# Layer 0 without a norm in front: transposed input times the gain goes into the projections, the root of the mean square is applied where they leave PSUM

## The chip, the core and the metric

The kernel runs on one core of one Trainium2 chip. The metric is the device time of one execution in microseconds (us); the times given are medians of several executions. The engines are TensorE (PE, matmuls, with its weight loads PEld), VectorE (DVE), ScalarE (ACT), GpSimd (POOL) and SyncE (SP), which here issues nearly all transfers. Each runs its own instructions in the order in which they were written, and waits for others by semaphores.

## What is computed

Two layers over 1024 tokens of width 1024, all in float32. The part that the change touches is the front of layer 0:

```python
def rms_norm(x, g):
    xf = x.astype(jnp.float32)
    y = xf * lax.rsqrt(jnp.mean(xf * xf, axis=-1, keepdims=True) + NORM_EPS)
    return (y * g.astype(jnp.float32)).astype(x.dtype)

h = rms_norm(x, norm_g[0])                       # layer 0
q, k, v, gate = jnp.split(h @ w_in, 4, axis=-1)  # mixer A: 16 heads of 64, each 1024 wide
# neighbourhood attention over a 16 x 64 grid: each query sees 8 x 16 keys, plus a bias per head
y = (o * silu(gate)) @ w_out
x = x + y
g = sigmoid(rms_norm(x, ple_norm_g[0]) @ ple_w_gate[0])
x = x + g * (p[0] @ ple_w_proj[0])
```

Layer 1 has the same frame with grouped-query attention, and one more norm ends the program. With r(t) = 1/sqrt(mean(x(t)^2) + eps) for token t, h(t) = r(t) * (x(t) * g), so that h @ w = r(t) * ((x * g) @ w): the factor r may be applied before the projection or behind it.

## The kernel before, in words

Every float32 product is made of three passes over operands split in a high and a low part: `HTh`, `HTl` hold the (normed) input transposed, [channel, token tile, channel block, token], and each weight unit of 128 x 1024 (512 KB) is split into `wh`, `wl`. The high part is made by ScalarE (a rounding copy), the low part by VectorE (the difference). `mm` (L303) issues all matmuls; `split3` is the three passes.

Weight units come through a queue, `Weights`: SP loads a unit into one of two staging buffers (`wstage`, L203), `pump` splits it (L218, L219). `pump` is called after each item of work, so transfers and splits are woven into the order in which the code is written; nothing else schedules.

`mixer_a` (layer 0) begins with the norm, by token tile t = 0..7 of 128 tokens: load `X[t]` [token, channel] (`load`, L694), ScalarE squares it with a running sum (`square`, L697), a mean on VectorE (L701), a power -1/2 on POOL (`rsqrt_ops`, L311), the scaling by r and gain (`scale`, L713 on VectorE or L715 and L716 on ScalarE and POOL), and eight PE transposes into PSUM, from where ScalarE and VectorE write `HTh` and `HTl` (`to_ht`, L413 to L415). Between these steps stand the projections of the first four heads' V, tile by tile (`v_items`, evictions L567 and L568). Then come q and k of head 0, transposed, in two halves of 512 tokens (`qk_items`, `qk_evac`: L581 copies PSUM to `th`, then `QS`, `KA`, `KB` are made; L590 and L593 copy halves of `KA` and `KB` across partitions).

Then the attention: for each head 8 steps of scores (`f_S`), exponent (`f_E`), transposes (`f_T`) and the product with V (`f_AV`). `mix` weaves the next head's q and k projections and the gate's (`gate_items`, L508) into them by cost. `table(h+1)` builds the next head's bias table on POOL (L612) from rows `u` that SP loads (L609) in step 1 of each head. These rows come from a table in DRAM that is built at the start by 8 and 16 small transfers (L748, L766). At the end of a head pair POOL multiplies the output with the gate and with the inverse row sums (`fin`, L499, L500), the latter spread by a trip through DRAM (L436, L438). Some steps are put off by a number of items with `post.add`; the q/k evictions' three steps by `QD = (2, 5, 8)`.

The first score matmul of head 0 is the first PE instruction behind the q and k of head 0.

## Time and profile before

| | |
|---|---|
| median of 3 runs | 1562.63 us (1560.91 to 1562.86) |
| the profiled execution, its own time | 1564.6 us |
| its span, from the first to the last instruction | 1562.8 us |
| mean granted TensorE clock | 0.997 |
| instructions | 23940 |

The page of a profile gives busy time by engine, then the span in 40 equal slices (a digit is the busy share in tenths). A timeline's row reads: start, duration, engine, line of the kernel, operation, output<-inputs, partitions x elements, how often, and in brackets how long the engine sat idle before it and what ended that. A row of a line's view gives the duration in ns as least/median/greatest, and the first and last start. A group's row (x31 | 18.4, 595 | 18.8 ...) gives the count, busy us, mean ns, and idle us before it with what ended it. A row of stretches gives start:end, length, then busy us (and instructions) of PE, PEld, DVE, ACT, POOL, the granted clock, the busy share of the DMA engines and GB/s.

### The profile page before, as it was taken

The numbers are of one execution on the slowest core, as the hardware profiler recorded it, in microseconds if no ns is written. First come the engines' busy times: TensorE is split into PE (matmuls) and PEld (weight loads), VectorE is DVE, ScalarE is ACT, GpSimd is POOL, SyncE is SP. The second block draws the span as 40 slices with busy tenths as digits, with TensorE's granted clock in tenths as the row PEclk, the third lists the DMA queues.
The fourth block names the chain that finished last, engine by engine and source line by source line (L and its number), as shares of the span: only waits on it lengthen the run. The fifth ranks groups of instructions, "written<-read, shape, count | busy, mean of one in ns | idle before, by whom it ended". The sixth has DMA issues, their size and how long they took to land.

```text
span 1562.8 us, 23940 instructions
## 1 busy us (share of the span) xinstructions
PE 1520.8 (97%) x9048; PEld 1328.0 (85%) x9048; DVE 965.3 (62%) x1660; ACT 871.6 (56%) x1744; POOL 320.3 (20%) x409
## 2 busy tenths in 40 slices
PE   6999999999999999999999999999999999999998
PEld 6888988988988788888988889989899888778886
DVE  5566576476467434536767776677777777624533
ACT  6565465466366523433566776776767777622422
POOL 3102102112012010000433142553141400000124
PEclk9999999999999999999999999999999999999999
DMA  8211222132122962132210111101101213651113
GB/s 288 83 40 53 66 67 78 40 93 79 40 80 83 340 237 90 53 130 104 77 49 22 38 51 42 59 24 55 50 27 46 77 39 107 233 202 54 68 59 130
DMA packets 89859, 138.82 MB, mean 89 GB/s; under 512 B 16913, under 2 KB 55953, under 8 KB 89745
## 3 DMA queue, kind: packets, MB, share of 16 engines
q1 hardware_dynamic: 85136, 122.62, 23.9%
q10 hardware_dynamic: 4608, 14.68, 2.6%
q8 instruction: 71, 1.16, 0.3%
q14 instruction: 44, 0.35, 0.1%
HBM read 104.65 MB, written 36.15 MB: 90 GB/s over the span
## 4 chain that ended last, share of the span: by engine, by line
PE 81%; ACT 6%; DVE 6%; issue 3%; POOL 2%; DMA 2%; SPq 0%; ACTq 0%; POOLq 0%; DVEq 0%
PE d L303 54%; PE o L303 10%; PE s L303 8%; PE t L1057 6%; PE t L654 2%; DVE PTl L1060 2%; PE t L413 2%; DVE mn L1041 1%; DMA wstage<-in_wts 1%; ACT PTh L1059 1%; ACT wh L218 1%; ACT P L1047 1%; POOL xn L402 1%; DVE wl L219 1%; POOL tb L612 1%
## 5 line engine op out<-in xcount | busy, mean ns | idle before, releaser
L303 PE MATMUL d<-wh,HTh 128*128 128x256 f32 (+1 forms) x1096 | 372.3, 340 | 4.9 <-ACT HTh L414 2.6
L303 PE MATMUL d<-wh,HTl 128*128 128x256 f32 (+1 forms) x1096 | 365.7, 334 | 1.5 <-DVE HTl L415 1.5
L303 PE MATMUL d<-wl,HTh 128*128 128x256 f32 (+1 forms) x1096 | 365.2, 333 | 0.0
L1060 DVE TENSOR_TENSOR PTl<-t,PTh 128x512 fp32r<-128x512 f32 x256 | 164.4, 684 | 123.4 <-ACT PTh L1059 122.8
L303 PEld LDWEIGHTS d<-wh,HTh 128*128 128x128 f32 x1096 | 207.7, 189 | 28.4 <-ACT HTh L414 3.2
L303 PEld LDWEIGHTS d<-wh,HTl 128*128 128x128 f32 x1096 | 207.7, 189 | 23.8 <-DVE HTl L415 2.1
L303 PEld LDWEIGHTS d<-wl,HTh 128*128 128x128 f32 x1096 | 208.0, 190 | 21.4
L303 PE MATMUL d<-HTh,wh 128*128 128x512 f32 x504 | 206.1, 409 | 0.0
L303 PE MATMUL d<-HTl,wh 128*128 128x512 f32 x504 | 197.7, 392 | 0.0
L303 PE MATMUL d<-HTh,wl 128*128 128x512 f32 x504 | 197.7, 392 | 0.0
L1047 ACT ACTIVATE P<-s,mn 128x1024 f32<-128x1024 f32 x128 | 142.8, 1115 | 58.3 <-DVE mn L1041 57.7
L1059 ACT ACTIVATE PTh<-t 128x512 fp32r<-128x512 f32 x256 | 139.9, 594 | 43.2 <-PE t L1057 42.3
L1041 DVE TENSOR_REDUCE mn<-s 128x1 f32<-128x1024 f32 x128 | 154.7, 1209 | 11.7 <-PE s L303 11.5
L1057 PE MATMUL t<-ident,P 128*128 128x128 f32 x1024 | 137.4, 275 | 6.7 <-DVE PTl L1060 4.8
L219 DVE TENSOR_TENSOR wl<-wstage,wh 128x1024 fp32r<-128x1024 f32 x89 | 113.8, 1284 | 39.9 <-ACT wh L218 39.4
L1057 PEld LDWEIGHTS t<-ident,P 128*128 128x128 f32 x1024 | 114.7, 141 | 22.5 <-DVE PTl L1060 16.5
L303 PE MATMUL s<-KA,QS 128*128 128x512 f32 (+2 forms) x384 | 133.7, 402 | 0.0
L303 PE MATMUL o<-PTh,V 128*128 128x256 f32 (+2 forms) x672 | 119.0, 288 | 3.3 <-ACT PTh L657 1.7
L303 PE MATMUL s<-KB,QS 128*128 128x512 f32 (+2 forms) x384 | 121.8, 371 | 0.0
L303 PE MATMUL o<-PTl,V 128*128 128x256 f32 (+2 forms) x672 | 119.5, 289 | 0.4 <-DVE PTl L658 0.3
L658 DVE TENSOR_TENSOR PTl<-t,PTh 128x384 fp32r<-128x384 f32 (+1 forms) x128 | 66.6, 520 | 79.3 <-ACT PTh L657 78.3
L303 PEld LDWEIGHTS d<-HTh,wl 128*128 128x128 f32 x504 | 94.6, 188 | 22.0
(159 smaller groups left out, 2456.7 us busy)
## 6 DMA issues: line engine op xcount, KB each, us to landing
wstage<-in_wts SPq DMA_DIRECT2D x92, 512.0 KB
X<-in_x SPq DMA_DIRECT2D x16, 512.0 KB
pp<-ppD SPq DMA_DIRECT2D x32, 256.0 KB
rb<-rD SPq DMA_DIRECT2D x56, 128.0 KB
ppD<-th SPq DMA_DIRECT2D x24, 256.0 KB
xD<-X SPq DMA_DIRECT2D x8, 512.0 KB
X<-xD SPq DMA_DIRECT2D x8, 512.0 KB
yD0h<-rb SPq DMA_DIRECT2D x14, 256.0 KB
```

Source lines behind the costliest of these rows:

```text
L218: act.activation(hi, s, AF.Copy)
L219: self.rest = lambda: dve.tensor_tensor(lo, s, hi, ALU.subtract)
L303: pe.matmul(ps, a, b, start=first, stop=last, skip_group_check=True)
L402: pool.tensor_scalar(xns[i][:, :512], xts[i][:, :512], r[:, i:i + 1], None, op0=ALU.mult)
L413: pe.transpose(ps[:, k], xn[:, (4 * c + k) * 128:(4 * c + k + 1) * 128], ident)
L654: pe.transpose(ps[:, i], sp[:, i * 128:(i + 1) * 128], ident)
L658: dve.tensor_tensor(PTl[:, sl], ps[:, :m], PTh[:, sl], ALU.subtract)
L1041: dve.tensor_reduce(mn, ps, axis=AX.X, op=ALU.min)
L1047: act.activation(p, ps, AF.Exp, bias=mn, scale=-1.0, accum_out=RS[h, hf][:, t:t + 1])
L1057: pe.transpose(ps[:, i], p[:, k * 128:(k + 1) * 128], ident)
L1059: act.activation(PTh[:, ks, c], ps, AF.Copy)
L1060: dve.tensor_tensor(PTl[:, ks, c], ps, PTh[:, ks, c], ALU.subtract)
```

## The change

The host now also gives x transposed (`xT`, channel by token), the gain of layer 0 as a column per channel block (`gain0`), and the bias rows per head ready made (`bias`) in place of the bias table.

The start of `mixer_a` is written anew. `put` multiplies a block of x^T by the gain per channel and writes the high part (ScalarE) and the low part (VectorE) of `HTh`, `HTl`, with neither norm nor transpose. The x tiles [token, channel] are still loaded, into four buffers, for the squares; `roots` makes r of four tiles at once (`rt`, a column per token tile), and `spread` transposes r on PE and copies it into `R` [any partition, token]. V of the first four heads is projected by halves of 512 tokens, channel block by channel block into two banks (`v_first`), and r comes in at the eviction (`v_evac`). Six times four transposes of the identity stand at PE's start. q, k and gates take R at their eviction, which moves from ScalarE to VectorE; the two copies across partitions move from VectorE to POOL. Each head's bias rows are loaded in step 0 and turned into the table in step 3.

```diff
-        "x": tokens(g["x"][0]), "wts": W, "rpb": rpb, "gains": gains, "hgains": hg,
+        "x": tokens(g["x"][0]), "xT": tokens(g["x"][0]).reshape(1024, 1024).T.reshape(8, 128, 1024), "wts": W, "bias": bias, "gains": gains, "gain0": g["norm_g"][0].reshape(8, 128).T, "hgains": hg,
...
+        def split_now(self, pieces):
+            key, pid = self.q[self.split]
+            s, _ = self.st.pop(key)
+            hi, lo = self.alloc[pid]()
+            for a, b in chunks(1024, 1024 // pieces):
+                act.activation(hi[:, a:b], s[:, a:b], AF.Copy)
+                dve.tensor_tensor(lo[:, a:b], s[:, a:b], hi[:, a:b], ALU.subtract)
...
     def gate_items(key, pair, hf, alloc, sb, gg, R=None):
...
-            act.activation(G, ps, AF.Copy)
+            if R is None:
+                act.activation(G, ps, AF.Copy)
+            else:
+                dve.tensor_tensor(G, ps, R[:, hf * 512:(hf + 1) * 512], ALU.mult)
...
+            def v_evac(t):
+                def evac(ps):
+                    v = ps.rearrange("p (h d) -> p h d", h=4)
+                    act.activation(V[:, t, :, 0:64], v, AF.Copy, scale=rt[:, t:t + 1])
+                    dve.scalar_tensor_tensor(V[:, t, :, 64:128], v, rt[:, t:t + 1], V[:, t, :, 0:64], op0=ALU.mult, op1=ALU.subtract)
+                return evac
...
+            def v_first(hf, banks, k):
+                wh, wl = WQ.get(("av", 0, k // 4))
+                c = slice((k % 4) * 256, (k % 4 + 1) * 256)
+                for i in range(3):
+                    for t in range(4):
+                        a = (HTh, HTh, HTl)[i][:, 4 * hf + t, k, :]
+                        mm(banks[t // 2][:, (t % 2) * 256:(t % 2 + 1) * 256], a, (wh, wl, wh)[i][:, c],
+                           k == 0 and i == 0 and t % 2 == 0, k == KC - 1 and i == 2)
...
-                    act.activation(raw, ps, AF.Copy)
+                    dve.tensor_tensor(raw, ps, R[:, s], ALU.mult)
...
-                        dve.tensor_copy(ka[lo, s], ka[hi, s])
+                        pool.tensor_copy(ka[lo, s], ka[hi, s])
...
-                        dve.tensor_copy(kb[lo, s], kb[hi, s])
+                        pool.tensor_copy(kb[lo, s], kb[hi, s])
...
+            def put(hf, k):
+                src = XT[hf][k // 2][:, k % 2].rearrange("p (t c) -> p t c", t=4)
+                ts = slice(4 * hf, 4 * hf + 4)
+                act.activation(HTh[:, ts, k, :], src, AF.Copy, scale=g0[:, k:k + 1])
+                dve.scalar_tensor_tensor(HTl[:, ts, k, :], src, g0[:, k:k + 1], HTh[:, ts, k, :], op0=ALU.mult, op1=ALU.subtract)
+
             def square(t):
-                act.activation(junk, X[t], AF.Square, accum_out=stat[:, 0, t:t + 1])
+                junk = ini.tile([128, D], BF16, name="junk")
+                act.activation(junk, X[t], AF.Square, accum_out=stat[:, t:t + 1])
...
+            def roots(hf):
+                c = slice(4 * hf, 4 * hf + 4)
+                dve.tensor_scalar(stat[:, c], stat[:, c], 1.0 / D, EPS, op0=ALU.mult, op1=ALU.add)
+                pool.tensor_tensor(rt[:, c], stat[:, c], neghalf[:, 0:4], ALU.pow)
+
+            def spread(hf):
+                ps = talloc()
+                for i in range(4):
+                    pe.transpose(ps[:, i], rt[:, 4 * hf + i:4 * hf + i + 1].to_broadcast([128, 128]), ident)
+                act.activation(R[:, hf * 512:(hf + 1) * 512], ps.rearrange("p t c -> p (t c)"), AF.Copy)
...
+            for i in range(6):
+                ps = talloc()
+                for j in range(4):
+                    pe.transpose(ps[:, j], ident, ident)
+            put(0, 0)
+            put(0, 1)
+            WQ.split_now(2)
+            put(0, 2)
+            put(0, 3)
+            WQ.split_now(1)
+            for k in range(4, KC):
+                put(0, k)
+            banks = [dalloc(), dalloc()]
+            for k in range(KC):
+                v_first(0, banks, k)
...
+            for t in range(4):
+                square(t)
+            roots(0)
+            for k in range(4):
+                put(1, k)
+            for t in range(4):
+                v_evac(t)(banks[t // 2][:, (t % 2) * 256:(t % 2 + 1) * 256])
+            for k in range(4, KC):
+                put(1, k)
+            WQ.split_now(1)
+            for t in range(4, NT):
+                square(t)
+            roots(1)
...
-            for d in qk_items(0):
+            for i, d in enumerate(qk_items(0)):
                 d[0]()
+                if i == 1:
+                    spread(1)
                 WQ.pump()
...
-                        if j == 1 and h + 1 < NH:
-                            table(h + 1)
+                        if h + 1 < NH:
+                            if j == 0:
+                                US[0] = bias_in(h + 1)
+                            if j == 3:
+                                table(h + 1, US[0])
```

From the last head pair's end on, the instructions of every engine stand in the same order as before. Where the order changes, three places are shown. SP, the start of the program, before (`X` is x by token tile, `gain` the broadcast gain, `wstage` a weight unit):

```order
L694 DMA X_109<-in_x 128x1024
L722 DMA gain<-in_gains 128x1024
L694 DMA X_110<-in_x 128x1024
L203 DMA wstage<-in_wts 128x1024 x2
L694 DMA X_111<-in_x 128x1024
L694 DMA X_112<-in_x 128x1024
```

SP, the same place, now (`g` is the gain by channel, `XT` two channel blocks of x^T for 512 tokens):

```order
L755 DMA g_110<-in_gain 128x8
L728 DMA XT_112<-in_xT 128x2x512
L205 DMA wstage<-in_wts 128x1024
L728 DMA XT_113<-in_xT 128x2x512
L205 DMA wstage<-in_wts 128x1024
L728 DMA XT_114<-in_xT 128x2x512
L728 DMA XT_115<-in_xT 128x2x512
L732 DMA X<-in_x 128x1024 x4
L728 DMA XT_116<-in_xT 128x2x512
```

The x tiles moved behind the first half of x^T and the two weight units of V. ScalarE, the start, before (`junk` is the square's output that nobody reads, `HTh` an eviction of transposes):

```order
L697 ACTIVATE junk,stat<-X_110 128x1024
L218 ACTIVATE wh_140<-wstage 128x1024
L218 ACTIVATE wh_146<-wstage 128x1024
L414 ACTIVATE HTh<-t 128x512 x2
L697 ACTIVATE junk,stat<-X_111 128x1024
L697 ACTIVATE junk,stat<-X_112 128x1024
```

ScalarE, the same place, now (`HTh<-XT,g` is `put`):

```order
L737 ACTIVATE HTh<-XT_112,g_110 128x4x128 x2
L232 ACTIVATE wh_178<-wstage 128x512 x2
L737 ACTIVATE HTh<-XT_113,g_110 128x4x128 x2
L232 ACTIVATE wh_188<-wstage 128x1024
L737 ACTIVATE HTh<-XT_114,g_110 128x4x128 x2
L737 ACTIVATE HTh<-XT_115,g_110 128x4x128 x2
L742 ACTIVATE junk,stat<-X 128x1024 x4
L737 ACTIVATE HTh<-XT_116,g_110 128x4x128 x2
L737 ACTIVATE HTh<-XT_117,g_110 128x4x128 x2
L583 ACTIVATE V<-d,rt 128x4x64 x4
```

The squares moved from in front of the first operands to between the two halves of them. POOL in the attention, before: the tables of heads 4 and 5 (`tb`) and the products at the end of the head pair before them (`Y`, one pair of rows for each half of the tokens); the like returns with the later heads:

```order
L612 TENSOR_TENSOR tb<-MK,u 128x128 x10
L499 TENSOR_TENSOR Y<-Y,G 128x512
L500 TENSOR_TENSOR Y<-Y,rb 128x512
L499 TENSOR_TENSOR Y<-Y,G 128x512
L500 TENSOR_TENSOR Y<-Y,rb 128x512
```

POOL, the same products and head 5's table, now (`KA`, `KB` are the copies across partitions for head 5, a pair for each half of its tokens):

```order
L513 TENSOR_TENSOR Y<-Y,G 128x512
L514 TENSOR_TENSOR Y<-Y,rb 128x512
L644 TENSOR_TENSOR tb<-MK,u 128x128 x5
L619 COPY KA<-KA 64x512
L622 COPY KB<-KB 64x512
L513 TENSOR_TENSOR Y<-Y,G 128x512
L514 TENSOR_TENSOR Y<-Y,rb 128x512
L619 COPY KA<-KA 64x512
L622 COPY KB<-KB 64x512
```

The copies moved into this queue, the first half's pair in front of the second pair of `Y` rows, the second half's behind it; and the table of head 5 stands behind the first pair.

136 lines of the change are left out of this document (54 added, 82 removed).

## The prediction

> **What bounds the kernel now.** I read the page first, for which engine fills the span.
>
> ```profile
> PE 1520.8 (97%) x9048; PEld 1328.0 (85%) x9048; DVE 965.3 (62%) x1660; ACT 871.6 (56%) x1744; POOL 320.3 (20%) x409
> ...
> PE   6999999999999999999999999999999999999998
> ...
> PEclk9999999999999999999999999999999999999999
> ```
>
> TensorE (PE) is busy 97% of the span, and in the row of forty slices of 39 us each only the first falls to 6. So two places can give time: the start, and the few microseconds of idle PE in the layer-0 attention behind it, the only other stage that the change edits. Next the start by stretches of 5 us (busy time of each engine, then clock, DMA share and GB/s):
>
> ```profile
> 0.00:5.00 5.00, 0.00 (x0) 0.00 (x0) 0.00 (x0) 2.15 (x2) 0.77 (x7) 1.00 0.66 185
> 5.00:10.00 5.00, 1.97 (x8) 1.57 (x8) 1.50 (x3) 2.49 (x5) 0.55 (x1) 1.00 1.01 400
> 10.00:15.00 5.00, 3.32 (x14) 3.09 (x15) 4.56 (x6) 4.22 (x7) 0.56 (x1) 1.00 1.02 419
> 15.00:20.00 5.00, 5.00 (x43) 4.84 (x42) 2.84 (x5) 4.38 (x8) 2.95 (x2) 1.00 1.08 356
> ...
> 30.00:40.00 10.00, 8.70 (x74) 8.50 (x73) 9.08 (x11) 5.69 (x10) 3.16 (x1) 1.00 0.91 278
> ```
>
> PE does 0, 2.0, 3.3 and 5.0 us of work in the four stretches, while from 5 us on the DMA share is full at 400 to 419 GB/s. (The last row is wanted further down.) Then the timeline of the start (start, duration, engine, line; in brackets the idle time before and what ended it):
>
> ```profile
> 4.13 1.06 ACT L697 ACTIVATE junk<-X 128x1024 bf16<-128x1024 f32 x1 [2.13 <-DMA X<-in_x]
> ...
> 7.61 1.06 ACT L697 ACTIVATE junk<-X 128x1024 bf16<-128x1024 f32 x1 [2.33 <-DMA X<-in_x]
> ...
> 7.75 1.97 PE L413 MATMUL t<-ident,X 128*128 128x128 f32 x8 [7.75 <-DVE X L713]
> ...
> 10.09 1.06 ACT L218 ACTIVATE wh<-wstage 128x1024 fp32r<-128x1024 f32 x1 [0.18 <-DMA wstage<-in_wts]
> ...
> 11.68 0.58 PE L303 MATMUL d<-wh,HTh 128*128 128x256 f32 x1 [1.96 <-ACT HTh L414]
> ...
> 13.22 0.41 PE L303 MATMUL d<-wh,HTl 128*128 128x256 f32 x1
> ...
> 13.43 0.41 PE L303 MATMUL d<-wh,HTh 128*128 128x256 f32 x1
> ```
>
> The first x tile is there by 4.13, the second (third in the queue) by 7.61, the second weight unit (fifth) by 10.06. PE gets its first transposes at 7.75, after square, root and scaling of tile 0, and its first projection matmul at 11.68. These first matmuls start 0.21 us apart (13.22, 13.43); later ones do better:
>
> ```profile
> 16.03 0.28 PE L303 MATMUL d<-wh,HTl 128*128 128x256 f32 x1
> ...
> 16.15 0.28 PE L303 MATMUL d<-wh,HTh 128*128 128x256 f32 x1
> ...
> 35.57 0.38 PE L303 MATMUL d<-wh,HTl 128*128 128x256 f32 x1 [1.30 <-DVE HTl L415]
> ...
> 45.78 0.40 PE L303 MATMUL d<-HTh,wh 128*128 128x512 f32 x1
> ...
> 56.69 0.28 PE L303 MATMUL s<-KA,QS 128*128 128x256 f32 x1
> ```
>
> From 16.0 us on V matmuls start 0.12 us apart. There is a stall of 1.30 us at 35.57, and 8 transposes stand in front of every token tile. V ends at 45.78, the 48 matmuls of head 0's q and k take 45.78 to 56.69 (0.227 each), and the first score matmul starts at 56.69. That is the mark I carry through: everything in front of it is rewritten, and what PE does behind it is the same list of matmuls.
>
> **The change, part by part.** All durations are of the one profiled execution (span 1562.8, its own time 1564.6, so 1.8 us lie around the span). The rows for the new steps are these:
>
> ```profile
> L697 ACT ACTIVATE junk<-X x8: 1054/1057/1066, 4.1 to 22.2; 128x1024 bf16<-128x1024 f32 x8
> L697 ACT ACTIVATION_READ_ACCUMULATOR junk<-X x8: 186/187/208, 5.1 to 23.2; 128x1 f32 x8
> L715 ACT ACTIVATE X<-X,stat x3: 1152/1152/1156, 16.5 to 29.4; 128x1024 f32<-128x1024 f32 x3
> L218 ACT ACTIVATE wh<-wstage x7: 1048/1057/1068, 8.8 to 58.8; 128x1024 fp32r<-128x1024 f32 x7
> L219 DVE TENSOR_TENSOR wl<-wstage,wh x6: 1209/1222/3077, 9.9 to 48.5; 128x1024 fp32r<-128x1024 f32 x6
> L415 DVE TENSOR_TENSOR HTl<-t,HTh x64: 675/691/694, 11.7 to 1484.6; 128x512 fp32r<-128x512 f32 x64
> L567 ACT ACTIVATE V<-d x32: 364/384/392, 21.0 to 432.3; 128x256 fp32r<-128x256 f32 x32
> 24.25 1.01 POOL L311 TENSOR_TENSOR stat<-stat,neghalf 128x4 f32<-128x4 f32 x1 [3.32 <-DVE stat L701]
> ```
>
> *Arrivals.* The queue now holds the small gain, x^T piece 0, V weights 0, x^T 1, V weights 1, x^T 2 and 3, four x tiles, four x^T pieces, head 0's weights, four x tiles: 19 pieces of 512 KB. The 4 KB in front costs one issue, some 0.45 us, so the first piece lands at 4.6; as before, the third comes 3.5 later and the rest every 1.23 ((10.06 - 7.61)/2, near 524 KB at 419 GB/s, 1.25). That gives weights 0 at 6.3, x^T 1 at 8.1, weights 1 at 9.3, the last x^T of the first half at 11.8, the fourth x tile at 16.7, x^T of the second half from 17.9 to 21.6, head 0's weights at 22.9, the last x tile at 27.8. Unknown is whether x^T, read in 2 KB pieces out of 4 KB rows, keeps that pace. Best: 1.23. Worst by a near row: 278 GB/s at share 0.91 in the stretch 30 to 40 us, where the bias tables move in pieces of 1.5 KB and less, so 305 GB/s and 1.72 us per x^T piece. I take 1.23: the fast stretches carry x, gain and weight tiles of 512 KB each, and an x^T piece is one transfer of that size.
>
> *First half of V.* x^T times gain and the split cost 0.6 to 0.7 us on ScalarE (half of L715's 1.15 is 0.58, plus fixed cost) and 0.69 on VectorE (L415). They don't wait for a root. The weights are split in two halves, 0.6 each, so PE starts at 6.3 + 0.6 = 6.9 in place of 11.68. It then needs 96 matmuls x 0.12 = 11.5 us, to 18.4. Nothing stops it on the way: the last put ends at about 11.8 + 3 x 0.7 = 13.9 and is needed at 17.0; the second weight unit's low half ends at 9.3 + 1.06 + 1.23 = 11.6, needed at 12.7.
>
> *Second half of V.* ScalarE takes the four squares ahead of it: 16.7 + 1.06 + 0.19 = 17.95, then the first put, 18.65. PE starts there, 0.25 us late, and runs 11.5 us, plus four transposes that spread r (0.5): 30.65. ScalarE meanwhile does 8 puts (5.6), 4 V evictions (L567, 1.5), a weight unit (1.06) and 4 squares (5.0): 31.1. VectorE's 0.16 and POOL's root of four columns (L311, 1.01) bring the second half's r at 32.4; PE asks for it after the first 12 q/k matmuls, at 33.4. One microsecond of slack, no cost.
>
> *Head 0.* 10.9 us of q and k matmuls and 0.5 for the second spread: first score at 42.05. The new reader of PSUM there, VectorE times R, is 0.69 where ScalarE took 0.60, and the copies end about 3.5 us after the first half's last matmul; 5.4 us of the second half cover that. Against 56.69 the start gives **14.6 us**: 4.8 by starting earlier, the other 9.8 from 64 transposes taken out (8 put in), stalls and half-speed matmuls. The 24 transposes of the identity cost nothing: at the slow 0.21 they take 5.0 us, and PE has nothing else before 6.9.
>
> *Steady state.* From the first score to 505 us:
>
> ```profile
> 56.69:505.00 448.31, 442.23 (x2542) 386.24 (x2540) 283.18 (x635) 260.64 (x579) 77.67 (x103) 1.00 0.21 64
> ```
>
> 448.31 less 442.23 leaves 6.1 us of idle PE. That bounds the gain there. Per head the change moves work between engines:
>
> ```profile
> L581 ACT ACTIVATE th<-d 128x512 f32<-128x512 f32 x31 | 18.4, 595 | 18.8 <-PE d L303 18.6
> L590 DVE CAST KA<-KA 64x512 fp32r<-64x512 f32 x31 | 15.5, 501 | 1.0
> L957 POOL CAST KA<-KA x8: 607/610/967, 769.8 to 1045.4; 64x512 fp32r<-64x512 f32 x8
> L612 POOL TENSOR_TENSOR tb<-MK,u 128x128 f32<-128x128 f32 x75 | 35.7, 511 | 333.5 <-DMA u<-U 255.5 <-DVE PTl L658 39.0 <-DVE Y L429 28.9
> ```
>
> ScalarE loses three evictions of 0.60 per head (-1.8), VectorE gains three of about 0.69 and loses four copies of up to 0.50 (-2.0): nothing, nearly. POOL gains four copies of 0.61: +2.4 of about 28 us. On VectorE the evictions queue behind other work, but ScalarE's rows show 18.6 us of waiting for PE, so the two buffers have room: one is wanted again only 24 matmuls (5.4 us) later. The bias rows are asked for at step 0 and used at step 3, where before POOL slept on them:
>
> ```profile
> 117.14 3.06 POOL L612 TENSOR_TENSOR tb<-MK,u 128x128 f32<-128x128 f32 x5 [35.14 <-DMA u<-U]
> 120.16 1.48 POOL L499 TENSOR_TENSOR Y<-Y,G 128x512 f32<-128x512 f32 x1
> 121.71 1.43 POOL L500 TENSOR_TENSOR Y<-Y,rb 128x512 f32<-128x512 f32 x1
> ...
> 124.83 0.55 PE L654 MATMUL t<-ident,sp 128*128 128x128 f32 x3 [1.29 <-ACT sp L646]
> ```
>
> Here the table was held by its transfer, the two Y products came behind it, ScalarE behind those, and PE lost 1.29 us. That knot alone is a fifth of the 6.1. With the rows early, the Y products are next to be late only when their own row sums come late. POOL's queue is what I checked for a new wait:
>
> ```profile
> 318.37 0.42 DVE L593 CAST KB<-KB 64x512 fp32r<-64x512 f32 x1
> ...
> 322.16 1.30 POOL L500 TENSOR_TENSOR Y<-Y,rb 128x512 f32<-128x512 f32 x1 [8.89 <-DMA rb<-rD]
> ...
> 323.55 0.36 PE L303 MATMUL s<-KA,QS 128*128 128x256 f32 x1
> ```
>
> Head 9's K copy ends at 318.79 and is wanted at 323.55: 4.8 us of slack. The POOL copies add 2 x 0.19, and a table in front of them 5 x 0.51 = 2.6: still in time. The Y product that waits until 322.16 for its transfer stands behind this copy in the new order. So the gain lies between -3.4 (copies behind that wait: 323.46 + 1.22 = 324.68, 1.1 late, at heads 5, 9 and 13) and 6.1; I take **1.0**, somewhat less than the knot shown: the order excludes the low end, and for the other idle no single cause is seen.
>
> *The bias table* no longer goes through DRAM: 24 small transfers leave SP and the queue. They lay beside PE's work, I count nothing. Sum: 14.6 + 1.0 = 15.6. The profiled execution would be 1564.6 - 15.6 = 1549.0; the median shown is 2.0 lower, so 1562.6 - 15.6 = **1547.0**.
>
> *A rule against it.* PE started its transposes at 7.75 and was at full pace only at about 15.7, 4 us after the first real matmul; between the two it idled 2 us. So the trace doesn't settle whether transposes bring up the pace (the page shows the granted clock as 9 throughout, it doesn't resolve this). If they don't, the first V matmuls run 0.21 apart for some 4 us again: 19 instead of 33, 14 x 0.12 = 1.7 us lost. The Trainium skill, "TensorE: Matmul & The Clock Gate", Part 4, says that transpose mode doesn't count as PE-busy in the same way, so full clock doesn't engage; Part 1 gives some 3.4 us of activity as the warm-up. By that rule the sum would be 13.9 and the time 1548.7. I hold the warm-up for somewhat likelier to work, since PE would be active from about 1 us on with hardly a pause. The Trainium skill, "DMA: Bandwidth & Descriptors", Specifications, gives 358 GB/s as the HBM limit of a core; the trace shows 419 over 5 us, and the measurement decides. By the page's figure, as an estimate, a piece takes 1.46, the fourth x tile and with it PE's second half come 7 x 0.23 = 1.6 us later, and the sum would be 14.0.
>
> **Rivals.** (1) *Half clock at first*: 1548.7, as above; for it, the 4 us behind 11.68; against it, the pause there. (2) *Copies late on POOL*: the 3.4 in place of the 1.0, 1551.4; the order speaks against it. (3) *The start becomes bound by transfers, slower*: the place is the last x tile, piece 19, whose r stops PE behind 12 q/k matmuls. First score = its landing + 2.6 (square, mean, root) + 0.5 + 36 x 0.227 = landing + 11.3. It turns slower when that passes 57.7, so a landing after 46.4, 2.32 us per piece or 226 GB/s. At 200 GB/s: landing 51.8, score 63.1, less 1.0 from the steady state: 1568. For it: 4 MB more are read. Against: 400 to 419 GB/s in the rows. (4) *The knots vanish whole*: 5 more, 1542. (5) *Nothing comes of it*: PE is earlier but then waits for head 1's weights, which are staged only when a buffer is free: 1562.6. Against it: they are asked for right behind the last x tile, which lands at 27.8, and wanted at 42.
>
> **How the numbers follow.** Forecast 0.56, (1) 0.20, (2) 0.08, (3) 0.03, (4) 0.09, (5) 0.04. A change under 0.2%, 3.1 us, can hardly be told from none. Faster 0.92 (forecast, 1, 2, 4 less a hundredth), same 0.05, slower 0.03. The low end is (4), 1542. The high end takes worst pace (2.1 later for the second half), half clock (1.7) and (2) (4.4) nearly together: 1553.5.
>
> **What would show it.** Right: first V matmul near 7, its neighbours 0.12 us apart; x^T-bound waits none after that; first score near 42; PE idle of the attention below 6 us; the rest of the trace merely shifted. Wrong: PE waiting for puts between 18 and 25 (slow x^T), 0.21 us between matmuls at 7 to 11, PE waiting for KA or KB from POOL, or VectorE late with a projection's eviction.

## The result and the profile after

| | before | after |
|---|---|---|
| runs, median us (lowest to highest) | 1562.64 (1560.91 to 1562.86, 4 runs) | 1545.41 (1544.8 to 1551.7, 4 runs) |
| profiled execution, us (its span) | 1564.6 (1562.8) | 1544.88 (1543.1) |

The ratio is 0.9900, 95% interval 0.9877 to 0.9923: 17.2 us faster by the medians, where 15.6 was forecast. That the sum came out so near is partly luck: the start gave less than forecast, the steady state more.

First the page of after: busy time by engine, the slices of 39 us, the granted clock.

```profile
PE 1513.8 (98%) x9016; PEld 1324.3 (86%) x9016; DVE 963.5 (62%) x1638; ACT 847.5 (55%) x1696; POOL 350.6 (23%) x468
...
PE   8999999999999999999999999999999999999998
...
PEclk9999999999999999999999999999999999999999
```

PE is at 98%, with 7 us less work in its row. The first slice rose from 6 to 8 tenths. Then the same four stretches of 5 us as before (length, then busy us of PE, PEld, DVE, ACT, POOL; clock, DMA share, GB/s):

```profile
0.00:5.00 5.00, 3.65 (x17) 3.66 (x18) 0.00 (x0) 0.00 (x0) 0.76 (x7) 1.00 0.55 141
5.00:10.00 5.00, 2.26 (x15) 2.02 (x14) 2.47 (x4) 4.51 (x7) 0.00 (x0) 0.84 1.03 409
10.00:15.00 5.00, 5.00 (x37) 5.00 (x37) 5.00 (x8) 4.97 (x9) 0.00 (x0) 0.82 1.04 412
15.00:20.00 5.00, 5.00 (x44) 5.00 (x43) 1.23 (x4) 4.84 (x9) 1.03 (x1) 1.00 1.04 390
```

PE works 3.65, 2.26, 5.0 and 5.0 us where it worked 0, 2.0, 3.3 and 5.0, though the 3.65 and about 0.9 of the 2.26 are transposes of the identity. The transfers kept their pace, 409 and 412 GB/s, so x^T out of 4 KB rows cost nothing that these stretches show. But the clock falls to 0.84 and 0.82. The timeline says why:

```profile
5.48 1.28 ACT L737 ACT_TABLE_LOAD   x1 [5.48 <-DMA XT<-in_xT]
6.77 1.33 ACT L737 ACTIVATE HTh<-XT,g 128x512 fp32r<-128x512 f32 x2
8.01 1.13 ACT L232 ACTIVATE wh<-wstage 128x512 fp32r<-128x512 f32 x2
...
8.68 1.22 PE L317 MATMUL d<-wh,HTh 128*128 128x256 f32 x4 [2.74 <-ACT wh L232]
9.70 1.12 PE L317 MATMUL d<-wl,HTh 128*128 128x256 f32 x4
...
12.11 0.64 PE L317 MATMUL d<-wl,HTh 128*128 128x256 f32 x4
...
21.70 0.64 PE L317 MATMUL s<-wh,HTh 128*128 128x256 f32 x4
...
33.64 0.40 PE L317 MATMUL d<-HTh,wh 128*128 128x512 f32 x1
...
45.02 0.28 PE L317 MATMUL s<-KA,QS 128*128 128x256 f32 x1
```

The first x^T piece lands at 5.48. Only then does ScalarE load its activation table, 1.28 us, and its first `put` runs at 6.77. Before, the same load stood at 0.72:

```profile
0.72 1.28 ACT L697 ACT_TABLE_LOAD   x1 [0.72 <-PEq L1294]
```

There too the first activation, the square at 4.13, waited for a transfer, but the load ran ahead of that wait. Why it stands behind the wait now is not shown; one difference is that a put reads two transfers, x^T and the gain, where the square reads one. Two puts, then the first half weight unit at 8.01, and PE's first V matmul at 8.68, after 2.74 us of idle. Its quadruples start 1.02 apart at 8.68 and 0.47 apart at 12.11: the first dozen matmuls ran at half pace, with a granted clock of 0.50:

```profile
9.00:10.00 1.00, 1.00 (x6) 1.00 (x6) 1.00 (x2) 1.00 (x3) 0.00 (x0) 0.50 1.06 412
10.00:11.00 1.00, 1.00 (x6) 1.00 (x6) 1.00 (x3) 1.00 (x2) 0.00 (x0) 0.50 1.07 416
11.00:12.00 1.00, 1.00 (x8) 1.00 (x7) 1.00 (x2) 1.00 (x3) 0.00 (x0) 0.59 1.04 412
12.00:14.00 2.00, 2.00 (x19) 2.00 (x18) 2.00 (x4) 2.00 (x4) 0.00 (x0) 1.00 1.03 412
```

V's second half starts at 21.70 without a wait, q and k at 33.64, the first score at 45.02 (56.69 before): **11.67 us**, not 14.6.

Behind it I compare the stretch from the first score to the first score of head 15, before and after:

```profile
56.69:502.75 446.06, 439.98 (x2527) 384.30 (x2526) 280.93 (x633) 258.41 (x574) 77.67 (x103) 1.00 0.21 64
45.02:486.48 441.46, 438.77 (x2527) 384.39 (x2526) 288.70 (x619) 236.39 (x531) 115.51 (x165) 1.00 0.22 67
```

446.06 became 441.46: **4.6 us**, not 1.0. PE's idle time in it fell from 6.08 to 2.69; the other 1.2 us are shorter busy time of the same 2527 matmuls. The gain comes in steps: head by head the distance between the kernels' first scores grows by 1.5 us over head 2, 0.8 over head 6, 1.7 over head 10 and 1.5 over head 14; over each of the others it changes by about 0.3 at most. In head 2, where before the table had stood ahead of the Y products, POOL now reads:

```profile
103.38 1.28 POOL L514 TENSOR_TENSOR Y<-Y,rb 128x512 f32<-128x512 f32 x1 [5.97 <-DMA rb<-rD]
104.62 2.15 POOL L644 TENSOR_TENSOR tb<-MK,u 128x128 f32<-128x128 f32 x5
106.83 0.98 POOL L619 CAST KA<-KA 64x512 fp32r<-64x512 f32 x1
```

The Y product of 103.38 waits for its own row sums alone, the table of 104.62 comes behind it and waits for nothing, and PE has no wait from 100 to 118. Together 16.3. The medians leave 0.9 more, the two profiled executions 3.4: from head 15's first score to the end they took 1060.05 and 1056.62 us. The instructions stand in the same order there, and in the fourteen profiled executions used in this text that part took 1055.8 to 1060.1, so it differs that much from one execution to the next.

### The profile page after: what moved, and what is told of

Read it like the earlier page. It is cut to its first block, busy times and chain, and to the rows that moved or that the text cites. A ratio compares the mean times of both kernels' runs of the same rounds, so it can differ in the third digit from the quotient of the medians.

```text
span 1543.1 us, 24012 instructions
## 1 busy us (share of the span) xinstructions
PE 1513.8 (98%) x9016; PEld 1324.3 (86%) x9016; DVE 963.5 (62%) x1638; ACT 847.5 (55%) x1696; POOL 350.6 (23%) x468
## 3 DMA queue, kind: packets, MB, share of 16 engines
q8 instruction: 71, 1.16, 0.3%
## 4 chain that ended last, share of the span: by engine, by line
PE 84%; DVE 6%; ACT 5%; issue 3%; DMA 1%; POOL 1%; ACTq 0%; POOLq 0%; SPq 0%; DVEq 0%
PE d L317 54%; PE o L317 10%; PE s L317 9%; PE t L1105 6%; PE t L686 2%; DVE PTl L1108 1%; PE t L427 1%; DVE mn L1089 1%; ACT PTh L1107 1%; DVE wl L221 1%; ACT P L1095 1%; ACT wh L220 1%; POOL xn L416 1%; PE t L1059 0%; DMA ppD<-G 0%
## 5 line engine op out<-in xcount | busy, mean ns | idle before, releaser
L317 PE MATMUL d<-wh,HTh 128*128 128x256 f32 (+1 forms) x1064 | 358.7, 341 | 5.3 <-ACT wh L232 2.7
L317 PE MATMUL d<-wh,HTl 128*128 128x256 f32 (+1 forms) x1064 | 352.2, 335 | 0.0
L317 PE MATMUL d<-wl,HTh 128*128 128x256 f32 (+1 forms) x1064 | 352.1, 335 | 0.0
L317 PEld LDWEIGHTS d<-wh,HTh 128*128 128x128 f32 x1064 | 200.0, 190 | 28.5 <-ACT wh L232 3.0
L317 PEld LDWEIGHTS d<-wl,HTh 128*128 128x128 f32 x1064 | 200.0, 190 | 21.4
L317 PEld LDWEIGHTS d<-wh,HTl 128*128 128x128 f32 x1064 | 199.8, 190 | 21.6
L221 DVE TENSOR_TENSOR wl<-wstage,wh 128x1024 fp32r<-128x1024 f32 x86 | 107.5, 1255 | 26.7 <-ACT wh L220 25.7
```

The costliest lines, as they stand in the source:

```text
L221: self.rest = lambda: dve.tensor_tensor(lo, s, hi, ALU.subtract)
L317: pe.matmul(ps, a, b, start=first, stop=last, skip_group_check=True)
```

## The experiments

The marks in the table are starts of first scores: of head 0, of head 1, and the stretch from head 0's to head 15's. Each mark is of one profiled execution. All but the first two rows are what the runs below gave. In the row with the scores early, head 0's mark stands ahead of the last quarter of its q and k, so it can't be compared with the others. The kernel before, rerun beside them, had medians of 1561.1 to 1562.6.

| kernel | time, us | head 0 | head 1 | stretch to head 15 |
|---|---|---|---|---|
| before | 1562.64 | 56.69 | 79.76 | 446.06 |
| after | 1545.41 | 45.02 | 68.26 | 441.46 |
| before, early rows | 1557.88 | 57.06 | 80.12 | 440.77 |
| before, early rows, copies on POOL | 1557.05 | 57.44 | 80.38 | 440.69 |
| after, copies on VectorE | 1549.51 | 45.27 | 69.01 | 445.36 |
| after, rows fetched beside the table | 1559.40 | 46.11 | 69.36 | 454.46 |
| after, 48 transposes | 1544.75 | 44.24 | 68.26 | 442.24 |
| after, early table load | 1544.96 | 43.85 | 68.17 | 442.26 |
| the same, no transposes | 1543.97 | 44.87 | 68.14 | 441.19 |
| the same, head 0's KB on VectorE | 1546.12 | 44.48 | 68.19 | 441.71 |
| that, and x^T ahead of x | 1547.39 | 43.59 | 70.04 | 444.48 |
| early load, squares shared | 1544.38 | 43.72 | 67.03 | 441.17 |
| that, head 0's KB on VectorE, scores early | 1544.92 | 42.86 | 67.35 | 442.41 |
| early load, squares shared, no transposes | 1543.31 | 44.18 | 67.42 | 441.21 |

The marks have a spread too. The kernel with the rows fetched beside the table has after's code up to head 0's scores, and yet its first score came at 46.11 in place of 45.02, behind a slow clock until about 14.5 us.

### The steady state: which part gave the 4.6 us

**Early rows alone**, in the kernel before (with the ready-made rows in the input and without the tables through DRAM; the diff shows the place of fetch and table):

```diff
-                        if j == 1 and h + 1 < NH:
-                            table(h + 1)
+                        if h + 1 < NH:
+                            if j == 0:
+                                US[0] = bias_in(h + 1)
+                            if j == 3:
+                                table(h + 1, US[0])
```

> The kernel before with only the bias part of the change: bias rows ready made in the input, asked for in step 0 of each head, the table built in step 3, no tables through DRAM. Theory (the rows' lateness made the knots at heads 3, 7, 11 and 15): first score stays near 56.7, and the attention from there to head 15's first score takes 441.5 in place of 446.1 us, PE idle there 2.7 in place of 6.1; time 1562.6 - 4.6 = 1558. Rival (the knots came from VectorE and ScalarE, and were undone by the moved evictions and copies): 446, idle 6, 1562.6.

Measured 1557.88 (1557.08 to 1560.23), ratio 0.9974 (0.9964 to 0.9984). The first score is 0.4 us later, the stretch:

```profile
57.06:497.83 440.77, 439.29 (x2527) 384.65 (x2526) 279.98 (x633) 259.11 (x575) 73.36 (x103) 1.00 0.20 65
```

440.77 and 1.48 us of idle: the ready-made rows, asked for early, take 5.3 us out of the stretch at once (4.1 by the medians of the whole). That is even a little more than the whole change got.

**Copies back on VectorE**, in the changed kernel:

```diff
-                        pool.tensor_copy(ka[lo, s], ka[hi, s])
+                        dve.tensor_copy(ka[lo, s], ka[hi, s])
...
-                        pool.tensor_copy(kb[lo, s], kb[hi, s])
+                        dve.tensor_copy(kb[lo, s], kb[hi, s])
```

> The changed kernel with the two copies across partitions back on VectorE. Theory (bias rows undid the knots, the copies don't matter): attention 441.5 us as in the changed kernel, first score within 0.5 of 45.0, 1545.4 within 1. Rival (VectorE's copies held by POOL, one of them 1.41 us in place of 0.42 before, were part of the knots): attention 443 to 446 us, 1547 to 1550. The rival on the other side (copies on POOL take 1.0 to 1.6 us and delay something): 440, 1544.

1549.51 (1548.42 to 1551.16), ratio 0.9923 (0.9908 to 0.9938), and the stretch:

```profile
45.27:490.63 445.36, 440.72 (x2528) 384.02 (x2526) 309.38 (x679) 235.50 (x528) 76.78 (x103) 1.00 0.21 67
```

445.36, the rival's outcome, with VectorE at 309 us of work in place of 289. In the changed kernel the copies on POOL are worth 3.9 us of the stretch, half of it idle PE and half longer busy time. Are they worth that by themselves, or do they only make room for the evictions? So **early rows and POOL copies in the kernel before**, evictions still on ScalarE:

```diff
-                        dve.tensor_copy(ka[lo, s], ka[hi, s])
+                        pool.tensor_copy(ka[lo, s], ka[hi, s])
...
-                        dve.tensor_copy(kb[lo, s], kb[hi, s])
+                        pool.tensor_copy(kb[lo, s], kb[hi, s])
```

> The kernel before with the bias rows ready-made and early, and the two copies of each half of k on POOL; its start and its evictions on ScalarE stay. Theory (the copies on POOL are worth 4 us only because the evictions of q, k and gates came to VectorE; without that VectorE has room): with PE idle already down to 1.5 us in the stretch from the first score to head 15's, which took 440.8 with the early rows alone, there is nothing left to take; the stretch is 440 to 441.5, time 1557 to 1558.5. Rival (the copies burden the chain of each score by themselves): the stretch falls to 437 to 439 and the time to 1554 to 1556.

1557.05 (1556.7 to 1557.58), ratio 0.9971 (0.9959 to 0.9983); the stretch from 57.44 to 498.13 is 440.69, against 440.77 without. So the copies on POOL give nothing by themselves; the evictions times R on VectorE cost some 4.6 (440.77 to 445.36), the copies' departure gives 3.9 back. The two kernels behind the 4.6 differ in their starts as well, so it isn't shown that all of it is the evictions'. All three sizes rest on one profiled execution of each kernel; the times agree with the 3.9 (1549.51 against 1545.41) and with the nothing (1557.05 against 1557.88).

**Rows fetched beside the table**, in the changed kernel. (The expectation's "as before the change" holds for the fetch standing just ahead of its table; the kernel before did both in step 1, this one does both in step 3.)

```diff
-                            if j == 0:
-                                US[0] = bias_in(h + 1)
                             if j == 3:
-                                table(h + 1, US[0])
+                                table(h + 1, bias_in(h + 1))
```

> The changed kernel, with each head's bias rows fetched in step 3, just ahead of the table, as before the change; still from the ready-made rows in the input. Theory (the place of the fetch made the 4 us of the early-rows run): the table on POOL waits for the rows again, and now KA's copy, on POOL since the change, queues behind that wait in the heads where the output work of two pairs is due; the stretch from the first score to that of head 15 grows from 441.5 to 446 or more, PE idle there from 2.7 to 6 or more, time 1549 to 1552. Rival (the source: rows ready-made in the input land sooner than rows cut from the table U): the stretch stays at 441 to 442.5, time 1545 to 1546.

1559.40 (1557.53 to 1563.15), ratio 0.9982 (0.9971 to 0.9993): 14 us lost, nearly the whole change, and far more than my 4 to 7. So the place of the fetch, with the copies queued behind the table, decides, ready-made rows or not; whether the source alone would help in step 1 wasn't tried. Rows of the timeline at head 5's start, SP's queue, then POOL, then PE, and the stretches around them; last, PE's row and a stretch at head 9's start:

```profile
184.44 1.09 SPq L452 DMA_DIRECT2D rb<-rD  x2
185.63 0.54 SPq L638 DMA_DIRECT2D u<-in_bias  x1
...
188.59 3.01 POOL L644 TENSOR_TENSOR tb<-MK,u 128x128 f32<-128x128 f32 x5 [20.74 <-DMA u<-in_bias]
191.67 0.61 POOL L619 CAST KA<-KA 64x512 fp32r<-64x512 f32 x1
...
192.33 0.58 PE L317 MATMUL s<-KA,QS 128*128 128x256 f32 x1 [2.91 <-POOL KA L619]
...
190.00:192.00 2.00, 0.00 (x0) 0.00 (x0) 0.61 (x2) 0.43 (x2) 1.94 (x5) 0.99 0.49 184
192.00:194.00 2.00, 1.67 (x4) 1.31 (x5) 0.43 (x2) 0.00 (x0) 1.92 (x3) 0.50 0.05 8
194.00:196.00 2.00, 2.00 (x7) 1.52 (x6) 0.00 (x0) 0.42 (x1) 1.86 (x3) 0.50 0.00 0
...
319.51 0.39 PE L317 MATMUL s<-KA,QS 128*128 128x256 f32 x1 [2.94 <-POOL KA L619]
...
320.00:322.00 2.00, 1.93 (x10) 1.68 (x11) 0.43 (x2) 0.00 (x0) 1.84 (x3) 1.00 0.00 0
```

On SP the fetch goes out at 185.63, behind the two transfers of `rb`. The table comes at 188.59, the KA copy behind it at 191.67, and PE, waiting 2.91 us for KA, starts the score at 192.33. This happens three times, at heads 5, 9 and 13, 8.7 us in sum. And behind head 5's pause the clock is at 0.50 until about 198, behind head 13's for some 3 us; behind head 9's, as long as the others (2.94), it stays at 1.00. PE's busy time in the stretch grew from 438.77 to 444.2. That second half of the bill I had not in my expectation: waits 7.6 more, busy time 5.4 more, together the 13.0 by which the stretch grew.

### The start: where 3 us went

**Early table load:** one small activation ahead of everything that waits.

```diff
+    warm = glob.tile([128, 32], F32, name="warm")
+    act.activation(warm, neghalf, AF.Square)
```

> The changed kernel with one small activation written ahead of everything, so that ScalarE's table load (1.28 us, from 5.48 in the changed kernel, behind the wait for the first x^T piece) comes at about 1.4. Theory (the table load lies on the start's path): first put at 5.5 in place of 6.77, first V matmul at 7.4 in place of 8.68, first score 1.3 us earlier than 45.02, 43.7; if the shorter pause of PE (5.95 to 7.4 in place of 8.68) also keeps its clock up, 12 V matmuls run 0.12 in place of 0.24 apart and the score comes at 42.3. Time 1542.6 to 1544.1. Rival (the first weight unit's arrival is the gate, the table load is hidden): first V matmul stays at 8.7, score at 45.0, 1545.4.

1544.96 (1544.27 to 1545.2), ratio 0.9892 (0.9877 to 0.9907). The table load, then rows of PE's timeline:

```profile
0.72 1.28 ACT L171 ACT_TABLE_LOAD   x1 [0.72 <-PEq L1343]
...
7.25 0.74 PE L319 MATMUL d<-wh,HTh 128*128 128x256 f32 x4 [0.60 <-ACT wh L234]
...
9.23 0.64 PE L319 MATMUL d<-wh,HTh 128*128 128x256 f32 x4
9.71 0.64 PE L319 MATMUL d<-wl,HTh 128*128 128x256 f32 x4
...
43.85 0.30 PE L319 MATMUL s<-KA,QS 128*128 128x256 f32 x1
45.31 0.38 PE L319 MATMUL s<-KB,QS 128*128 128x256 f32 x1 [1.16 <-POOL KB L624]
```

The first V matmul comes at 7.25 in place of 8.68, behind a pause of 0.60 only, and the clock stays at 1.00. But V's second half now waits 1.0 us for HTh, whose x^T has not landed; the first score is 1.2 us earlier, at 43.85, and its second matmul waits 1.16 for the KB copy of POOL. Head 1 starts at 68.17 against 68.26: the gain is gone again.

**48 transposes** in place of 24, with the table load where the change has it:

```diff
-            for i in range(6):
+            for i in range(12):
```

> The changed kernel with 48 in place of 24 transposes of the identity at PE's start, which at the pace of the last ones (0.11) end near 8.6 in place of 5.95, so PE has no pause before the first V matmul at 8.68. Theory (the transposes do bring the clock up, and the pause of 2.7 us lets it fall): the first 12 V matmuls run 0.12 in place of 0.24 apart, granted clock 1.0 from 5 to 15 us, first score 1.4 us earlier, 43.6; 1544.0. Rival (transposes don't hold the clock; it comes up only by projection matmuls): V's first 12 matmuls stay slow, score 45.0, 1545.4. If the transposes overshoot, the first V matmul comes up to 0.5 us late.

1544.75 (1543.84 to 1545.37), ratio 0.9891 (0.9876 to 0.9906). The transposes last until 9.5, V begins at 9.27 at full pace with no fall of the clock, and the first score comes at 44.24: 0.59 us later than after's first matmul, 0.78 earlier at the first score. So what cost after its pace was the pause, not the late arrival alone: about 1.4 us. Head 1 again starts at 68.26.

**No transposes**, with the early table load (the six groups at PE's start are left out):

> The run with the early table load, without the 24 transposes of the identity at PE's start. Theory (transposes count as work that keeps or brings the clock up): the first V matmuls, at 7.2, go 0.24 apart with a granted clock of 0.5 for some 3 to 4 us; V's first half ends about 1.5 to 2 later than with the transposes, the first score at 44.5 to 45.5, and the time is 1545.0 to 1546.5. Rival (the chip's clock does not count transposes; it was the length of PE's pause alone that set it): the same 0.12 apart from the start, or the same slow stretch with and without transposes.

1543.97 (1543.16 to 1545.94), ratio 0.9885 (0.9870 to 0.9900).

```profile
7.45 1.22 PE L319 MATMUL d<-wh,HTh 128*128 128x256 f32 x4 [7.45 <-ACT wh L234]
8.46 1.13 PE L319 MATMUL d<-wl,HTh 128*128 128x256 f32 x4
```

Four matmuls take about 1 us here and 0.48 in the run with transposes (9.23, 9.71 above), from the same start within 0.2 us: the transposes do bring the pace up. The Trainium skill, "TensorE: Matmul & The Clock Gate", Part 4, says that full clock doesn't engage in transpose mode; these two runs show otherwise for transposes of an identity in f32. Yet the time is not longer: the first score comes 1.02 later, head 1's at the same place.

**What sets head 1's start.** In four of the kernels so far the first score comes between 43.85 and 45.02, and head 1's between 68.14 and 68.26. In after and in the run without transposes head 1 follows the first score by 23.24 and 23.27; in the two with an earlier first score it follows by 24.02 and 24.32, so there something else holds it. Two attempts to use the earlier PE, both with the early table load. **Head 0's KB on VectorE:**

```diff
-                        pool.tensor_copy(kb[lo, s], kb[hi, s])
+                        (dve if h == 0 else pool).tensor_copy(kb[lo, s], kb[hi, s])
```

> The run with the early table load, and head 0's KB copies back on VectorE. Theory (the 2.8 us won at the start were spent in waits, 1.2 of it the first score waiting for the KB copy that took 1.61 on POOL): the 1.2 us wait goes, the first score of head 1 comes at 67.0 instead of 68.2, time 1543.8. Rival (something further down, a weight or the output work, sets head 1's start in all three runs): the first score of head 1 stays at 68.1 to 68.3 and the time at 1545.

1546.12 (1545.33 to 1547.82), ratio 0.9898 (0.9883 to 0.9913). The wait for KB is gone, head 1 stays at 68.19: the rival's outcome. This profiled run had a slow start (a pause of 1.48 before the first V matmul, then a clock of 0.50 for some 3 us) and still met the same mark. It also shows what a pause costs late, at the end of head 15 (PE's row, and the stretches around it):

```profile
520.11 0.45 PE L319 MATMUL o<-PTh,V 128*128 128x384 f32 x1 [2.13 <-ACT PTh L691]
...
515.00:518.00 3.00, 2.97 (x19) 2.38 (x17) 0.91 (x3) 0.89 (x3) 0.00 (x0) 1.00 1.04 415
518.00:521.00 3.00, 0.58 (x2) 0.32 (x2) 1.26 (x4) 1.46 (x3) 0.00 (x0) 0.97 1.03 411
521.00:524.00 3.00, 3.00 (x9) 2.52 (x10) 0.36 (x1) 0.82 (x2) 0.00 (x0) 0.50 1.04 419
524.00:527.00 3.00, 2.31 (x12) 1.52 (x10) 2.07 (x3) 1.57 (x4) 0.00 (x0) 0.96 1.03 415
```

A wait of 2.13 for PTh, and the next 3 us run at 0.50. The second, **x^T ahead of x**, comes on top of the first:

```diff
+            load_t(1, 0)
             for t in range(4):
                 load(t)
-            for i in range(4):
+            for i in range(1, 4):
                 load_t(1, i)
...
+            for k in range(2):
+                put(1, k)
             for t in range(4):
                 square(t)
...
-            for k in range(4):
+            for k in range(2, 4):
                 put(1, k)
```

> The kernel of the run with early table and KB copies on VectorE, with the first piece of the second half of x^T loaded ahead of the four x tiles, and its two puts ahead of the squares. Theory (V's second half waits 1.0 us for HTh because its x^T lands at 19.7, after the x tiles): that wait falls to 0.3 or less, first score 0.7 to 1.0 earlier than without, time 1542.9. Rival (the r factors, whose squares now come later, or the V eviction gate q and k instead): the first score stays within 0.3 of the run without, time 1543.8.

1547.39 (1546.46 to 1548.99), ratio 0.9906 (0.9891 to 0.9921): slower than the early load alone (at most 1545.2), though not clearly slower than the run with KB on VectorE. The wait of 1.0 for HTh at the start of V's second half is gone, one of 0.4 comes later in it, and the first score came 0.26 earlier than with the early load alone, but head 1 came at 70.04:

```profile
55.08 0.55 PE L688 MATMUL t<-ident,sp 128*128 128x128 f32 x3 [1.71 <-ACT sp L680]
...
56.00:58.00 2.00, 1.20 (x5) 1.11 (x6) 1.67 (x4) 1.16 (x5) 1.21 (x3) 0.75 0.40 162
58.00:60.00 2.00, 2.00 (x6) 1.52 (x6) 0.56 (x1) 0.68 (x3) 1.53 (x4) 0.50 0.03 8
```

PE, earlier, ran out of work sooner; it waited 1.71 for a softmax that came no earlier, and paid with the clock. That points to the chain on ScalarE and VectorE. Its head is in the squares of the second half: in the early-load run ScalarE's last square of 32.37 ends at 33.5, and root, V's evictions, R, a weight split and head 0's q and k stand behind it. **Squares shared**, with the early load and KB on POOL again, moves two of these four to VectorE:

```diff
+                if t in (5, 7):
+                    dve.tensor_tensor_reduce(out=X[t], in0=X[t], in1=X[t], scale=1.0, scalar=0.0, op0=ALU.mult, op1=ALU.add, accum_out=stat[:, t:t + 1])
+                    return
```

> The run with the early table load, with the squares of x tiles 5 and 7 on VectorE (idle there from 30.2 to 33.6) in place of ScalarE. Theory (not PE but the chain of ScalarE and VectorE from the squares over r, the V evictions, R and the weight split to the first softmax sets head 1's start, which is why a first score from 43.6 to 45.0 all came out at 68.1 to 68.3): the last square ends 2 us earlier, V's second evictions and head 0's first half of q and k too, so the first score's wait of 1.2 for KB goes, the first reduction comes at 47.3 instead of 47.96, head 1's first score at 67.0 to 67.6, time 1543.9 to 1544.4. Rival (the chain from the last q and k matmul, with nothing of it earlier, sets it): head 1 at 68.1, time 1545.0.

1544.38 (1543.26 to 1547.81), ratio 0.9885 (0.9867 to 0.9903). The first V eviction of the second half, here and (second row) in the early-load run:

```profile
33.74 0.48 ACT L585 ACTIVATE V<-s,rt 128x256 fp32r<-128x256 f32 x1 [2.25 <-POOL rt L752]
...
34.85 0.48 ACT L585 ACTIVATE V<-s,rt 128x256 fp32r<-128x256 f32 x1 [0.84 <-POOL rt L749]
```

1.1 us earlier, not 2: the two squares take VectorE 1.2 each, one after the other. Head 1 starts at 67.03, 1.14 earlier, though the first score moved by only 0.13. So with the early load the chain is shown to set it. And 67.03 is 23.31 behind the first score, near the 23.24 of after: now head 1 hangs on the first score again. **Scores early** goes on, with head 0's KB copies on VectorE too:

```diff
                 WQ.pump()
+                if i == 6:
+                    f_S(0, 0)
+                    f_E(0, 0)
+                    f_S(0, 1)
...
-            f_S(0, 0)
-            f_E(0, 0)
-            f_S(0, 1)
```

> The run with shared squares, head 0's KB copies on VectorE, and the first two scores and the first exponential put ahead of the last quarter of head 0's q and k. Theory (head 0's first steps have no projection work between scores and transposes to hide the chain of reduction, exponential and weight splits, and PE idles 1.2 to 2.5 us at 54 to 58): the first reduction comes near 43 instead of 48, PE's idle at 54 to 58 falls to 0.5 or less, head 1's first score at 66.0 to 66.8, time 1542.5 to 1543.5. Rival (the two weight splits of 2.3 us each on VectorE and ScalarE at 50 to 53.5 make that wait, wherever the scores stand): PE idle stays over 1 us there and head 1 at 67 or later, time 1544.

1544.92 (1543.76 to 1546.69), ratio 0.9884 (0.9868 to 0.9900), head 1 at 67.35: nothing won. The first reduction came at 44.27 instead of 47.18, but the second weight split on VectorE at 51.37 instead of 51.05 and PE's wait of 0.82 at 55 remained. For head 1 that is the rival's outcome, though its wait of over 1 us is not; a wait of 0.82 or 0.83 for the softmax stands at this place of head 0 in every profiled execution of this text. The rival's cause, the weight splits there, wasn't tried alone. Last, **squares shared without transposes:**

> The run with shared squares, without the 24 transposes at PE's start. Theory (PE's start is not what head 1 waits for): V begins at half pace for 4 us and the first score comes 0.8 to 1.2 later, at 44.5 to 44.9, but head 1's first score stays at 66.9 to 67.3 and the time at 1543 to 1545. Rival (with the chain of squares shortened PE's own start decides): head 1's first score comes 0.8 or more later, at 67.8 or after.

1543.31 (1542.7 to 1545.47), ratio 0.9885 (0.9868 to 0.9901), head 1 at 67.42. It is the lowest median of the study, 2.1 below the changed kernel's, but the intervals overlap. V ran at half pace for 4.5 us, the first score came 0.46 later than with transposes, head 1 0.39 later, 23.24 behind the first score. That is the rival's mechanism at a smaller size than it gave: with the chain shortened, PE's own start decides. The times can't confirm any of this: the variants of the start win 1.2 us at most at head 1, and the part behind head 15 alone differs by up to 4.3 from one execution to the next.

## Why the prediction came out right

*Arrivals.* The pace held in GB/s, and no put but the first waited for x^T in after. The first piece came at 5.48 in place of 4.6: I had put 0.45 for the one more issue ahead of it; it was three times that (1.35). Later pieces can be late as well: in the early-load run the first x^T piece of the second half came at 19.68, where I had 17.9, and PE waited 0.98 for it. After's late PE hid that.

*First half of V.* This step failed: PE was to start at 6.9 and started at 8.68. Its working left out the activation table. The load was in the trace of before, at 0.72, hidden there; now it stands behind the wait for the first transfer. The early-load run gives back 1.43 us of the 1.78. The rest goes with the late first piece: in that run the two puts that stand ahead of the weight split start at 5.34. Then 96 matmuls took 13.0 us (8.68 to 21.70), not 11.5. "With hardly a pause" was wrong, since 2.74 us of pause lay between transposes and V.

*Second half of V* and *Head 0.* With PE 3 us late nothing was late any more: no gate at the puts (0.25 was forecast), V's second half with the spread took 11.94, q and k with the second spread 11.38, as forecast. The start gave 11.67 in place of 14.6, and 1.78 (first matmul) + 1.5 (pace) - 0.25 (gate) makes up the difference of about 3. With PE on time, the step would have failed elsewhere: in the early-load run the squares' chain, which I had given 1 us of slack, sets head 1's start.

*Steady state.* The term was undersized: 1.0 taken, 4.6 measured. I priced one knot out of at least four and held that "for the other idle no single cause is seen"; the row of POOL's table, with 255.5 us of waiting for `u`, was the common cause, and the early-rows run removes it but for 1.5 us of idle. "Nothing, nearly" for the moved evictions and copies holds as a sum (0.7 by 441.46 against 440.77), but as 4.6 lost and 3.9 won back. Rival (4), the knots vanish whole, is nearly what happened there (4.6 of the 6.1), with a start worse than forecast.

*Rivals (1) and (2).* The half clock came, with 1.5 where 1.7 was priced, but from the pause, not from transposes that don't count. Copies late on POOL did not occur in the steady state of after; with the rows late they did, at the heads 5, 9 and 13 that the low end had named, and cost far more than its 1.1 each. Two errors with opposite signs, 2.9 too much at the start and 3.6 too little behind it, leave 1547.0 against 1545.41; that they nearly cancel is luck.

## What to carry to other kernels

ScalarE's first activation brings fixed work with it, here a table load of 1.28 us, and that can fall behind the wait for a transfer (5.48 in after) or ahead of it (0.72 in before): read in the trace where it stands. A small first activation on data that is there early moved it ahead. When an in-order queue holds a fetch and its use side by side, count every place where they recur before pricing one. And price a PE pause with the pace that may follow it, not by its length alone.

## What the runs showed of the hardware that I had not expected

Short pauses of PE often brought the granted clock down. Pauses of 1.48, 1.71, 1.75, 2.13, 2.43, 2.74, 2.90, 2.91 and 2.96 us were followed by 0.50, for some 3 to 6 us. The length alone does not decide it: head 9's pause of 2.94 in the run with the rows beside the table kept 1.00, so did a pause of 1.53 to 1.61 in layer 1 (1334.33 in after) in all fourteen profiled executions, and in the run with the scores early three pauses of 0.38, 0.42 and 0.70 close together, at 760.72 to 762.49, were followed by 0.50. What else decides is open. The Trainium skill, "TensorE: Matmul & The Clock Gate", Part 1, puts the fall behind an idle window of some 3.4 us; here half of that could be enough.

The recorded clock does not show the first warm-up: without transposes the matmuls from 7.45 to about 12.8 us ran at half pace with 1.00 on record, so the distance between starts has to be read as well.

POOL's copy of 64x512 took 0.61 us at the least, 0.78 at the median of the changed kernel, and 1.61 in the early-load run beside a weight split on VectorE (the durations of one line, then two rows of the timeline):

```profile
L619 POOL CAST KA<-KA x32: 607/777/1325, 42.0 to 477.3; 64x512 fp32r<-64x512 f32 x32
...
43.65 1.61 POOL L624 CAST KB<-KB 64x512 fp32r<-64x512 f32 x1
...
43.56 1.22 DVE L223 TENSOR_TENSOR wl<-wstage,wh 128x1024 fp32r<-128x1024 f32 x1 [0.33 <-ACT wh L222]
```

The Trainium skill, "SBUF — State Buffer", SBUF: two separate sides, says that a VectorE operation with two SBUF operands and a GpSimd one that reads SBUF exclude each other for their whole length; the split ends at 44.78, the copy 0.48 later, so the trace agrees as far as one pair of rows can.
